# Strassen's scheme for most of the gate and up products of four feed-forward stages in a fused float32 model kernel

## The chip, the cores and the metric

One core of a Trainium2 chip runs one launch of a whole small model. The metric is the device time of a launch in microseconds (us). TensorE is called PE, VectorE DVE, ScalarE ACT, GpSimd POOL, SyncE SP.

## What is computed

256 tokens of width 1024 go through four transformer layers in float32. Each layer has attention (or a mixer of three branches) and then a feed-forward stage with a hidden width of 2816; the last two layers add a gated embedding. The change concerns the feed-forward stages:

```python
FFN_HIDDEN = 2816                                       # D_MODEL = 1024, SEQ = 256
h = rms_norm(x, ffn_norm[layer])
gate, up = jnp.split(h @ w_gate_up[layer], 2, axis=-1)  # 256 x 1024 by 1024 x 5632
x = x + (jax.nn.silu(gate) * up) @ w_down[layer]        # 256 x 2816 by 2816 x 1024
```

There are four of them: `w_gate_up[0]`, `w_gate_up[1]`, `w_gate_up_2[0]`, `w_gate_up_2[1]`, all of the same size.

## The kernel before

**Products.** PE multiplies in a rounded float32 (`F32R`). To keep the accuracy every operand is split in a high and a low part, and each block product is three matmuls (`mm3`, lines 250 to 252): high by high, high by low, low by high. Activations are the stationary operand (128 tokens), weights the moving one (128 x 512). `Weight.split` makes the two parts of a raw weight block of 128 x 1024: ACT copies it rounded into `wh` (line 236), DVE subtracts, `wl = wr - wh` (line 237, both inputs in SBUF). `split_T` (line 269 on) transposes activations on PE and makes their two parts, on ACT from PSUM and on DVE from PSUM.

**Feed-forward stage** (`ffn`, line 466 on). Gate and up weights are packed in eleven chunks; chunk c has 256 gate and the matching 256 up columns. `up(c)` loads and splits four weight blocks, and for each half t of the tokens runs `dense`: 8 parts of the inner width x 3 matmuls into one PSUM bank (`psb`). ACT takes Silu of the gate half (`sg`, line 483), DVE multiplies by the up half (`h`, line 485). `turn(c)` transposes `h` into `hth` and `htl` (lines 493 to 497). `down(c)` takes two blocks of `w_down` of 128 x 1024 each and accumulates into four PSUM banks that live for the whole stage (two `psd`, two `psm`). The order is up(c), turn(c-1), down(c-2); the last two chunks' down products come at the end, bank by bank, so that the first bank's sum can go on early.

**What sets the order.** The code gives a program order; a planner (a list scheduler with a time model of its own) puts the instructions of each engine into a fixed order from it. Loads are kept in program order on SP's queue. At run time each engine works through its own list in order and waits on semaphores. Buffers belong to tags with a fixed number each (`BUFS`, line 155); a tile waits until one of its tag is free: five raw blocks `wr`, five each of `wh` and `wl`, 14 of `rg`, 8 of `vv`, 2 of `acc`, 4 of `qkT`. POOL does small work: sums for the norms, rotary additions (line 419), the merging of the mixer's branches (line 1068); it takes no part in the feed-forward products.

Of the kernel before, what the change touches and what calls it, by code (L numbers as in the profile page):

```python
# [51 lines left out]
GU_CHUNKS = [_cols((256 * c, 256 * c + 256), (FFN + 256 * c, FFN + 256 * c + 256)) for c in range(11)]  # L52
# [95 lines left out]
def model(ctx: ExitStack, tc: tile.TileContext, A, out, taps=None):  # L148
# [67 lines left out]
    def raw_block(src, off, n):  # L216
        raw = tmp([BLK], "wr", "wr")
        load(raw[:, :n], bass.AP(tensor=src.tensor, offset=src.offset + off, ap=[[n, P], [1, n]]))
        return raw

    class Weight:
# [8 lines left out]
        def load(self, k0, m, n, off):  # L230
            return k0, m, n, raw_block(self.src, self.base + off, m * n)[:, :m * n]
# [233 lines left out]

    def ffn(nm, w_gu, gu_base, w_dn, dn_base, after):
# [6 lines left out]
        hT = {}  # L473

        def up(c):
            w = gu.get(c)
            hs = []
            for t in range(2):
# [7 lines left out]
                hs.append(h)  # L486
            return hs

        def turn(c, hs):
            pt = psb()  # L490
            for t in range(2):
                for j in range(2):
                    nc.tensor.transpose(pt[:, j * 256 + t * P:j * 256 + (t + 1) * P], hs[t][:, j * P:(j + 1) * P], ident)  # L493
            hi, lo = tmp([2, 256], "xt", "hth", F32R), tmp([2, 256], "xt", "htl", F32R)
            v = pt.rearrange("p (j t) -> p j t", j=2)
            nc.scalar.activation(hi, v, AF.Copy)
            nc.vector.tensor_tensor(lo, v, hi.bitcast(F32), op=ALU.subtract)
            hT[c] = (hi, lo)
# [3 lines left out]
        def down(c, toks, cols=(0, 1)):  # L502
            if c not in dw:
                dw[c] = dn.block(*dn.by[0][2 * c]) + dn.block(*dn.by[0][2 * c + 1])
            hi, lo = hT[c]
            for t in toks:
                ts = slice(t * P, (t + 1) * P)
                for n in cols:
                    for k, wh, wl in dw[c]:
                        j = k - 2 * c  # L510
                        s = slice(n * 512, n * 512 + 512)
                        mm3(acc[t, n], hi[:, j, ts], lo[:, j, ts], wh[:, s], wl[:, s], c == 0 and j == 0, c == 10 and j == 1)

        hs = {0: up(0)}
        for c in range(1, 11):
            hs[c] = up(c)
            turn(c - 1, hs.pop(c - 1))
            if c >= 2:
                down(c - 2, (0, 1))
        turn(10, hs.pop(10))  # L520
        for t in range(2):
            for n in range(2):
                down(9, (t,), (n,))
                down(10, (t,), (n,))
# [23 lines left out]
    def layer0(nm, after):  # L548
# [7 lines left out]
        vt = [tmp([3, 2, 65], "vv", "vt") for _ in range(2)]  # L556
# [8 lines left out]
        qp, qr, qb = ([tmp([2, 256], "rg", nm_) for _ in range(2)] for nm_ in ("qp", "qr", "qb"))  # L565
# [17 lines left out]
        def keys_T(dup):  # L583

            z = tmp([2, 256], "rg", "kz")
# [9 lines left out]
        def dup_tile(name):  # L595
            return tmp([2, 2, 64], "vv", name)
# [6 lines left out]
        ksd, kwd, bkd, kcd, vcd = [], [], [], [], []  # L603
        for t in range(2):
# [6 lines left out]
            kcd.append(dup_tile("kcd"))  # L611
# [6 lines left out]
        kz = {0: keys_T(ksd)}  # L618
# [49 lines left out]
        def chunk2():  # L668

            w = win.get(2)  # L670
# [678 lines left out]
```

## Time and profile before

| | |
|---|---|
| median of 3 runs | 1595.64 us (1594.61 to 1598.0) |
| the profiled run's own time | 1594.98 us |
| its span | 1593.1 us |
| instructions | 21691 |
| read from HBM | 267 MB, 168 GB/s over the span |
| loads of `w_gate_up` | 176 of 512 KB |

The profile is one execution. A row of busy time counts the time in which an engine has an instruction under way; matmuls are pipelined, so that two rows overlap, and the distance of their starts is the pace. "Idle before" is what the engine stood still ahead of an instruction, with what ended that. A weight load (PEld) overlaps the matmuls.

### The profile page before, as it was taken

The numbers are of one execution on the slowest core, as the hardware profiler recorded it, in microseconds if no ns is written. First come the engines' busy times: TensorE is split into PE (matmuls) and PEld (weight loads), VectorE is DVE, ScalarE is ACT, GpSimd is POOL, SyncE is SP. The second block draws the span as 40 slices with busy tenths as digits, with TensorE's granted clock in tenths as the row PEclk, the third lists the DMA queues.
The fourth block names the chain that finished last, engine by engine and source line by source line (L and its number), as shares of the span: only waits on it lengthen the run. The fifth ranks groups of instructions, "written<-read, shape, count | busy, mean of one in ns | idle before, by whom it ended". The sixth has DMA issues, their size and how long they took to land.

```text
span 1593.1 us, 21691 instructions
## 1 busy us (share of the span) xinstructions
PE 1561.7 (98%) x7870; PEld 1314.3 (82%) x7870; DVE 978.9 (61%) x1770; ACT 856.8 (54%) x1385; POOL 140.3 (9%) x231
## 2 busy tenths in 40 slices
PE   8999999999999999999999999999999999999997
PEld 7777888899888888798878888888898778888886
DVE  6685545577665555675686655457576776554556
ACT  5545444454554444676574654446675474644445
POOL 2010000011100000120023000000120023000001
PEclk9999999999999999999999999999999999999999
DMA  7424555544545565452556555564552555465661
GB/s 268 155 84 143 194 184 181 183 149 131 171 146 186 184 197 185 140 187 79 172 160 225 171 187 186 184 198 159 164 173 87 184 186 178 161 203 184 198 203 56
DMA packets 80588, 269.53 MB, mean 169 GB/s; under 512 B 11361, under 2 KB 12769, under 8 KB 80481
## 3 DMA queue, kind: packets, MB, share of 16 engines
q1 hardware_dynamic: 80048, 267.10, 51.6%
q8 instruction: 62, 1.02, 0.3%
q10 hardware_dynamic: 432, 1.05, 0.2%
q14 instruction: 46, 0.37, 0.1%
HBM read 267.06 MB, written 1.05 MB: 168 GB/s over the span
## 4 chain that ended last, share of the span: by engine, by line
PE 93%; DVE 3%; ACT 2%; issue 1%; DMA 1%; POOL 0%; POOLq 0%; SPq 0%; DVEq 0%; ACTq 0%
PE psd L250 14%; PE psd L252 14%; PE psd L251 14%; PE psb L252 10%; PE psb L250 10%; PE psb L251 10%; PE psb L357 5%; PE psm L251 3%; PE psm L250 3%; PE psm L252 3%; PE psb L374 1%; DVE wl L237 1%; PE psb L493 1%; PE psb L269 1%; PE psm L269 1%
## 5 line engine op out<-in xcount | busy, mean ns | idle before, releaser
L237 DVE TENSOR_TENSOR wl<-wr,wh 128x1024 fp32r<-128x1024 f32 (+2 forms) x504 | 596.7, 1197 | 425.1 <-ACT wh L236 411.1
L236 ACT ACTIVATE wh<-wr 128x1024 fp32r<-128x1024 f32 (+2 forms) x504 | 512.5, 1031 | 456.6 <-PE psb L252 176.9
L250 PE MATMUL psd<-wh,th 128*128 128x512 f32 (+4 forms) x888 | 336.1, 381 | 7.3 <-DVE gt L1049 5.2
L252 PE MATMUL psd<-wh,tl 128*128 128x512 f32 (+4 forms) x888 | 332.9, 376 | 3.4 <-DVE tl L278 3.4
L251 PE MATMUL psd<-wl,th 128*128 128x512 f32 (+4 forms) x888 | 333.3, 376 | 0.8 <-DVE wl L237 0.8
L252 PE MATMUL psb<-wh,tl 128*128 128x512 f32 x720 | 275.0, 390 | 0.0
L251 PE MATMUL psb<-wl,th 128*128 128x512 f32 x720 | 274.5, 389 | 0.0
L250 PE MATMUL psb<-wh,th 128*128 128x512 f32 x720 | 274.0, 390 | 0.0
L250 PEld LDWEIGHTS psd<-wh,th 128*128 128x128 f32 x888 | 167.5, 189 | 34.4 <-DVE gt L1049 4.5
L252 PEld LDWEIGHTS psd<-wh,tl 128*128 128x128 f32 x888 | 167.3, 188 | 29.4 <-DVE tl L278 5.0
L251 PEld LDWEIGHTS psd<-wl,th 128*128 128x128 f32 x888 | 167.5, 189 | 25.0 <-DVE wl L237 1.6
L252 PEld LDWEIGHTS psb<-wh,tl 128*128 128x128 f32 x720 | 135.2, 188 | 28.1
L251 PEld LDWEIGHTS psb<-wl,th 128*128 128x128 f32 x720 | 135.2, 188 | 28.0
L250 PEld LDWEIGHTS psb<-wh,th 128*128 128x128 f32 x720 | 135.2, 188 | 27.6
L305 POOL TENSOR_SCALAR rest<-ss 128x1 f32<-128x1 f32 x24 | 7.2, 301 | 919.0 <-ACT junk L315 919.0
L366 ACT ACTIVATE pr<-pr,m 128x128 f32<-128x128 f32 (+1 forms) x144 | 58.4, 449 | 40.7 <-DVE m L365 39.1
L250 PE MATMUL psd<-wh,hth 128*128 128x512 f32 x176 | 71.9, 412 | 0.0
L483 ACT ACTIVATE sg<-psb,r 128x256 f32<-128x256 f32 x88 | 41.9, 476 | 52.6 <-PE psb L252 52.5
L251 PE MATMUL psd<-wl,hth 128*128 128x512 f32 x176 | 68.8, 391 | 0.0
L251 PE MATMUL psm<-wl,hth 128*128 128x512 f32 x176 | 68.5, 389 | 0.0
L250 PE MATMUL psm<-wh,hth 128*128 128x512 f32 x176 | 68.5, 389 | 0.0
L252 PE MATMUL psm<-wh,htl 128*128 128x512 f32 x176 | 67.8, 389 | 0.0
(322 smaller groups left out, 1762.4 us busy)
## 6 DMA issues: line engine op xcount, KB each, us to landing
wr<-w_gate_up SPq DMA_DIRECT2D x176, 512.0 KB, 4.3
wr<-w_down SPq DMA_DIRECT2D x88, 512.0 KB, 3.3
wr<-w_in SPq DMA_DIRECT2D x88, 512.0 KB, 4.1
wr<-w_qkv_o SPq DMA_DIRECT2D x32, 384.0 KB, 3.4
wr<-w_o SPq DMA_DIRECT2D x16, 512.0 KB, 4.2
wr<-w_ple_gate SPq DMA_DIRECT2D x16, 512.0 KB, 3.8
wr<-w_in_e SPq DMA_DIRECT2D x10, 512.0 KB, 4.8
wr<-w_out_e SPq DMA_DIRECT2D x8, 512.0 KB, 4.7
```

Of the source, the lines that this page charges most:

```text
L236: nc.scalar.activation(hi[:, :m * n], raw, AF.Copy)
L237: nc.vector.tensor_tensor(lo[:, :m * n], raw, hi[:, :m * n].bitcast(F32), op=ALU.subtract)
L250: nc.tensor.matmul(o, xh, wh, start=start, stop=False)
L251: nc.tensor.matmul(o, xh, wl, start=False, stop=False)
L252: nc.tensor.matmul(o, xl, wh, start=False, stop=stop)
L269: nc.tensor.transpose(p[:, j * P:(j + 1) * P], src[:, j * P:(j + 1) * P], ident)
L305: nc.gpsimd.tensor_scalar(rest, ms, self.eps, None, op0=ALU.add)
L357: mm = lambda o, l, r, a, b: nc.tensor.matmul(o, l, r, start=a, stop=b, skip_group_check=True)
L366: exps.append(nc.scalar.activation(e, e, AF.Exp, bias=neg, scale=-1.0))
L374: nc.tensor.transpose(bank[j][:, b * P:(b + 1) * P], pr[:, j, b * P:(b + 1) * P], ident)
L483: nc.scalar.activation(sg, o[:, :256], AF.Silu, scale=r)
L493: nc.tensor.transpose(pt[:, j * 256 + t * P:j * 256 + (t + 1) * P], hs[t][:, j * P:(j + 1) * P], ident)
```

## The change

Eight of the eleven chunks are taken in four pairs. A pair has 512 gate and 512 up columns. With A the activations cut in two halves of tokens and two halves of the inner width, and B the pair's weights cut in two halves of the inner width and into gate and up, the four result blocks (two halves of tokens, gate and up) are made by Strassen's scheme (in Winograd's form): seven block products of 128 tokens x 512 inner x 512 columns in place of eight. Four of the seven weight operands are sums or differences of weight blocks (`t1` to `t4`), made by POOL (`combine`) ahead of the split; four activation operands are sums (`ms`), made once per stage (`mixed`: POOL adds, ACT and DVE split). The seven products share three PSUM banks, and ACT and DVE read partial sums between them. Parts 0, 5 and 6 of the seven `PARTS` stay as they were (`plain`). `down` goes by single blocks of 128 hidden columns, and `seven` and `plain` call `fill()` to place a `turn` or a `down` between two products.

For the room the buffer tags are cut anew: `rg`, `vv`, `acc`, `qkT` and `cm` become `ra` (7 buffers of 1024 columns) and `sb` (8). Attention and mixer tiles are taken from these two, most of them as a `duo`: two halves of one buffer, which come free together. Raw blocks of a pair come from `ra`, combined ones from `sb`.

```diff
+PARTS = [(0, 256), (256, 512), (768, 512), (1280, 512), (1792, 512), (2304, 256), (2560, 256)]
...
-    BUFS = {"wr": 5, "wh": 5, "wl": 5, "xt": 16, "rg": 14, "acc": 2, "w512": 5, "qkT": 4, "pr": 2, "pt": 2, "vv": 8, "fa": 4, "qk": 2, "ow": 2, "junk": 1, "cm": 1, "w128": 4}
+    BUFS = {"wr": 5, "wh": 5, "wl": 5, "xt": 16, "ra": 7, "sb": 8, "w512": 5, "pr": 2, "pt": 2, "fa": 4, "qk": 2, "ow": 2, "junk": 1, "w128": 4}
...
+    def duo(shape, tag, name, dt=F32):
+
+        t = tmp([2] + list(shape), tag, name, dt)
+        return [t[:, 0], t[:, 1]]
...
+    def combine(x, y, op):
+
+        k0, m, n, v = x
+        z = tmp([BLK], "sb", "wt")
+        nc.gpsimd.tensor_tensor(z, v, y[3], op=op)
+        return k0, m, n, z
...
+        def mixed():
+
+            f = lambda x: x.bitcast(F32)
+            tok = {}
+            for t, n in ((1, 0), (1, 1), (0, 0), (0, 1)):
+                hi, lo = nm.h[t, n]
+                tok[t, n] = tmp([4, P], "w512", "xa")
+                nc.gpsimd.tensor_tensor(tok[t, n], f(hi), f(lo), op=ALU.add)
+            s1, s2, s3, s4 = tok[1, 1], tok[0, 0], tok[1, 0], tok[0, 1]
+            nc.gpsimd.tensor_tensor(s1, tok[1, 0], tok[1, 1], op=ALU.add)
+            nc.gpsimd.tensor_tensor(s3, tok[0, 0], tok[1, 0], op=ALU.subtract)
+            nc.gpsimd.tensor_tensor(s2, s1, tok[0, 0], op=ALU.subtract)
+            nc.gpsimd.tensor_tensor(s4, tok[0, 1], s2, op=ALU.subtract)
...
+            for j, v in ((2, s2), (3, s3), (1, s1), (4, s4)):
+                hi, lo = ms[j] = to[j]
+                nc.scalar.activation(hi, v, AF.Copy)
+                nc.vector.tensor_tensor(lo, v, f(hi), op=ALU.subtract)
+
+        def product(o, x, blocks, start, stop):
+            w = sum((gu.split(b) for b in blocks), [])
+            for j, (_, wh, wl) in enumerate(w):
+                mm = [(x[0], wh), (x[0], wl), (x[1], wh)]
+                for e, (l, r) in enumerate(mm):
+                    nc.tensor.matmul(o, l[:, j, :], r, start=start and j == 0 and e == 0, stop=stop and j == 3 and e == 2, skip_group_check=True)
...
+            for e in range(2):
+                b11[e] = ld(g[e])
+            for e in range(2):
+                b12[e], b22[e] = ld(u[e]), ld(u[2 + e])
+            for e in range(2):
+                b21[e] = ld(g[2 + e])
+            for e in range(2):
+                t3[e] = combine(b22[e], b12[e], ALU.subtract)
+                t2[e] = combine(t3[e], b11[e], ALU.add)
+                t1[e] = combine(b12[e], b11[e], ALU.subtract)
+            for e in range(2):
+                t4[e] = combine(b21[e], t2[e], ALU.subtract)
+            r = nm.rstd
+            new = lambda: tmp([512], "w512", "hx")
+            A_, B_, F_ = psb(), psb(), psb()
+            product(A_, nm.h[0, 0], b11, True, False)
+            h0 = new()
+            nc.scalar.activation(h0, A_, AF.Copy)
+            fill()
+            product(B_, nm.h[0, 1], b21, True, True)
+            nc.vector.tensor_tensor(h0, h0, B_, op=ALU.add)
+            nc.scalar.activation(h0, h0, AF.Silu, scale=r[0])
+            if not ms:
+                mixed()
+            product(A_, ms[2], t2, False, False)
+            h1 = new()
+            nc.scalar.activation(h1, A_, AF.Copy)
+            fill()
+            product(F_, ms[3], t3, True, False)
+            product(A_, ms[1], t1, False, False)
+            u1 = new()
+            nc.scalar.activation(u1, A_, AF.Copy)
+            nc.vector.tensor_tensor(u1, u1, F_, op=ALU.add)
+            fill()
+            product(A_, ms[4], b22, False, True)
+            nc.vector.scalar_tensor_tensor(h0, A_, r[0], h0, op0=ALU.mult, op1=ALU.mult)
+            fill()
+            product(F_, nm.h[1, 1], t4, False, True)
+            nc.vector.tensor_tensor(h1, h1, F_, op=ALU.add)
+            nc.scalar.activation(h1, h1, AF.Silu, scale=r[1])
+            nc.vector.scalar_tensor_tensor(h1, u1, r[1], h1, op0=ALU.mult, op1=ALU.mult)
...
-            ksd.append(dup_tile("ksd"))
...
-        accA, accB = (tmp([2, 512], "acc", "acc") for _ in range(2))
+        accA, accB = (tmp([2, 512], "sb", "acc") for _ in range(2))
...
+            pw[0, n], pw[1, n] = duo([512], "ra", "pw")
...
-                pw[t, n] = tmp([512], "rg", "pw")
```

## Rows read from the trace of the kernel before

**Rows 1.** The page, part 1: busy us (share) x instructions
```profile
PE 1561.7 (98%) x7870; PEld 1314.3 (82%) x7870; DVE 978.9 (61%) x1770; ACT 856.8 (54%) x1385; POOL 140.3 (9%) x231
```
**Rows 2.** The page, part 4: the chain that ended last, by engine
```profile
PE 93%; DVE 3%; ACT 2%; issue 1%; DMA 1%; POOL 0%; POOLq 0%; SPq 0%; DVEq 0%; ACTq 0%
```
**Rows 3.** Windows of first and last feed-forward stage: PE, PEld, DVE, ACT, POOL; clock; DMA
```profile
143.00:329.00 186.00, 186.00 (x848) 153.93 (x847) 101.16 (x120) 89.39 (x121) 1.97 (x6) 1.00 0.56 184
...
1373.00:1559.00 186.00, 186.00 (x845) 153.87 (x844) 98.48 (x108) 88.86 (x114) 0.98 (x3) 1.00 0.58 190
```
**Rows 4.** Waits of the first feed-forward stage: us, times, longest
```profile
DVE wl L237 <- ACT wh L236: 74.2, 30, 4.0
...
ACT wh L236 <- PE psb L252: 43.4, 30, 4.3
```
**Rows 5.** Timeline of PE in the first stage: start us, us, instruction
```profile
203.66 0.39 PE L250 MATMUL psb<-wh,th 128*128 128x512 f32 x1
...
204.34 0.62 PE L250 MATMUL psb<-wh,th 128*128 128x512 f32 x2
```
**Rows 6.** The chain in that stage, longest pieces: start us, us
```profile
204.51 0.45 PE psb L250 x2
...
238.11 0.45 PE psb L250 x2
```
**Rows 7.** Groups of DVE by form: busy us, mean ns, idle before
```profile
L237 DVE TENSOR_TENSOR wl<-wr,wh 128x1024 fp32r<-128x1024 f32 x442 | 536.3, 1226 | 392.9 <-ACT wh L236 379.1
...
L526 DVE TENSOR_TENSOR x<-x,psd 128x512 f32<-128x512 f32 x8 | 5.5, 688 | 1.6 <-PE psd L252 1.6
...
L1139 DVE SCALAR_TENSOR_TENSOR ug<-ug,rgt 128x512 f32<-128x512 f32 x4 | 2.5, 668 | 0.0
```
**Rows 8.** Groups of ACT by form
```profile
L236 ACT ACTIVATE wh<-wr 128x1024 fp32r<-128x1024 f32 x442 | 461.8, 1059 | 413.6 <-PE psb L252 176.9 <-PE psm L252 145.5 <-PE psd L252 80.3
...
L928 ACT ACTIVATE u<-psd,r 128x512 f32<-128x512 f32 x4 | 2.8, 691 | 9.8 <-PE psd L252 9.8
```
**Rows 9.** Timeline of POOL: additions of 128 and 512 columns; 512 with one source
```profile
41.58 0.46 POOL L419 TENSOR_TENSOR kr<-ra,rb 128x128 f32<-128x128 f32 x1 [0.67 <-DVE rb L418]
...
818.71 1.04 POOL L1133 TENSOR_TENSOR rgt<-xc 128x512 f32<-128x512 f32 x1 [0.88 <-ACT xc L1130]
...
853.56 1.29 POOL L1068 TENSOR_TENSOR gt<-gt 128x512 f32<-128x512 f32 x1 [28.06 <-DVE gt L1064]
```
**Rows 10.** Timeline: POOL starts just after `wl`
```profile
873.50 1.22 DVE L237 TENSOR_TENSOR wl<-wr,wh 128x1024 fp32r<-128x1024 f32 x1
873.73 2.13 POOL L1068 TENSOR_TENSOR gt<-gt 128x512 f32<-128x512 f32 x1 [2.52 <-DVE gt L1064]
```
**Rows 11.** Timeline: `wl` starts just after POOL
```profile
718.22 0.46 POOL L419 TENSOR_TENSOR qtok<-ra,rb 128x128 f32<-128x128 f32 x1 [4.18 <-DVE rb L418]
718.28 1.48 DVE L237 TENSOR_TENSOR wl<-wr,wh 128x1024 fp32r<-128x1024 f32 x1
```
**Rows 12.** Timeline: a DVE operation that reads PSUM while POOL works
```profile
862.36 3.46 POOL L1068 TENSOR_TENSOR gt<-gt 128x512 f32<-128x512 f32 x2 [1.99 <-DVE gt L1064]
863.39 0.69 DVE L1064 TENSOR_TENSOR gt<-psd,gt 128x512 f32<-128x512 f32 x1
```
**Rows 13.** Timeline at the start of the first stage
```profile
142.84 11.92 SPq L176 DMA_DIRECT2D wr<-w_gate_up  x5
...
147.67 2.15 DVE L278 SCALAR_TENSOR_TENSOR tl<-psm,S,th 128x128 fp32r<-128x128 f32 x8
```
**Rows 14.** The page, part 6: loads, KB each, us to landing
```profile
wr<-w_gate_up SPq DMA_DIRECT2D x176, 512.0 KB, 4.3
```
**Rows 15.** Windows (columns as in rows 3) and timeline around a wait in a mixer
```profile
1296.00:1300.00 4.00, 2.04 (x9) 1.40 (x8) 4.00 (x7) 4.00 (x7) 0.00 (x0) 1.00 0.18 74
1300.00:1304.00 4.00, 4.00 (x12) 3.09 (x12) 4.00 (x8) 1.62 (x4) 0.00 (x0) 0.57 0.64 166
...
1299.23 0.50 PE L250 MATMUL psd<-wh,th 128*128 128x512 f32 x1 [1.96 <-DVE gt L1049]
```

More of the change, by code (lines that the diff above doesn't have):

```diff
@@ L51 @@
 ] + [_cols((3240 + 512 * j, 3752 + 512 * j)) for j in range(6)]
-GU_CHUNKS = [_cols((256 * c, 256 * c + 256), (FFN + 256 * c, FFN + 256 * c + 256)) for c in range(11)]
+PARTS = [(0, 256), (256, 512), (768, 512), (1280, 512), (1792, 512), (2304, 256), (2560, 256)]
+GU_CHUNKS = []
+for _a, _n in PARTS:
+    _g, _u = (_a, _a + _n), (FFN + _a, FFN + _a + _n)
+    GU_CHUNKS += [_cols(_g, _u)] if _n == 256 else [_cols(_g), _cols(_u)]
 HALVES = [_cols((0, 512)), _cols((512, 1024))]
@@ new lines, in product, with seven @@
+        def product(o, x, blocks, start, stop):
[4 more added lines that the diff above has]
+                    nc.tensor.matmul(o, l[:, j, :], r, start=start and j == 0 and e == 0, stop=stop and j == 3 and e == 2, skip_group_check=True)
+        def seven(i, c, fill):
+            g, u = gu.by[c], gu.by[c + 1]
+            ld = lambda b: gu.load(*b, tag="ra")
+            b11, b12, b21, b22, t1, t2, t3, t4 = ([None, None] for _ in range(8))
+            for e in range(2):
[34 more added lines that the diff above has]
+            nc.vector.scalar_tensor_tensor(h0, A_, r[0], h0, op0=ALU.mult, op1=ALU.mult)
+            fill()
+            product(F_, nm.h[1, 1], t4, False, True)
+            nc.vector.tensor_tensor(h1, h1, F_, op=ALU.add)
+            nc.scalar.activation(h1, h1, AF.Silu, scale=r[1])
+            nc.vector.scalar_tensor_tensor(h1, u1, r[1], h1, op0=ALU.mult, op1=ALU.mult)
+            hs[i] = [h0, h1]
@@ L506, in down, with turn @@
+        def turn(i):
+            n = PARTS[i][1] // P
+            hT[i] = [split_T(h, n) for h in hs.pop(i)]
+        dw = {}
+        def down(i, k, toks, cols):
+            if k not in dw:
+                dw[k] = dn.block(*dn.by[0][k])[0][1:]
+            wh, wl = dw[k]
+            j = k - PARTS[i][0] // P
             for t in toks:
-                ts = slice(t * P, (t + 1) * P)
+                hi, lo = hT[i][t]
                 for n in cols:
[L509 to L520, printed above, removed]
+                    s = slice(n * 512, n * 512 + 512)
+                    mm3(acc[t, n], hi[:, j, :], lo[:, j, :], wh[:, s], wl[:, s], k == 0, k == FFN // P - 1)
+        def kts(i):
+            return [(i, k) for k in range(PARTS[i][0] // P, sum(PARTS[i]) // P)]
+        end = kts(len(PARTS) - 2) + kts(len(PARTS) - 1)
@@ new lines, in ffn, with fill @@
+        c = 0
+        for i, (a, n) in enumerate(PARTS):
+            todo = []
+            if i:
+                todo.append(lambda: turn(i - 1))
+            if i > 0:
+                todo += [lambda i_=i_, k=k: down(i_, k, (0, 1), (0, 1)) for i_, k in kts(i - 1) if (i_, k) not in end]
+            def fill():
+                if todo:
+                    todo.pop(0)()
+            (plain if n == 256 else seven)(i, c, fill)
+            while todo:
+                fill()
+            c += 1 if n == 256 else 2
@@ L521, in ffn @@
+        turn(len(PARTS) - 1)
         for t in range(2):
             for n in range(2):
-                down(9, (t,), (n,))
-                down(10, (t,), (n,))
+                for i, k in end:
+                    down(i, k, (t,), (n,))
                 s = slice(n * 512, n * 512 + 512)
@@ L555, in layer0 @@
         load(w2v, A["cmp_v_w2"])
-        vt = [tmp([3, 2, 65], "vv", "vt") for _ in range(2)]
+        vt = duo([3, 2, 65], "sb", "vt")
         for t in range(2):
@@ L670, in chunk2 @@
             w = win.get(2)
+            kwd, bkd = (dup_tiles(n_) for n_ in ("kwd", "bkd"))
             for t in range(2):
@@ L987, in branch @@
         def branch(qt, kt, v, dk, mask):
-            o = tmp([2, 512], "acc", "acc")
+            o = tmp([2, 512], "sb", "acc")
             for j in range(4):
-                s = [heads_T(lambda t: qt(t, 2 * j + h), lambda t: kt(t, 2 * j + h), dk) for h in range(2)]
+                s = duo([2, 256], "ra", "qkT")
+                for h in range(2):
+                    heads_T(s[h], lambda t: qt(t, 2 * j + h), lambda t: kt(t, 2 * j + h), dk)
                 pov, _ = attend(lambda h: s[h][:dk, 0], lambda h: s[h][:dk, 1], lambda kt_, h: v[kt_][:, 2 * j + h, :], mask)
@@ L1075, in mixer @@
         sigmoids = gate(2, of_attention)
-        uT = [tmp([2, 259], "vv", "uT") for _ in range(2)]
+        uT = duo([2, 259], "sb", "uT")
         for a in range(2):
@@ L1080, in mixer @@
         channels(5, lambda a, t, v: nc.vector.tensor_copy(uT[a][:, :, 3 + t * P:3 + (t + 1) * P], v))
-        ug = [tmp([2, 256], "rg", "ug") for _ in range(2)]
+        ug = duo([2, 256], "ra", "ug")
         channels(6, lambda a, t, v: nc.vector.tensor_copy(ug[a][:, :, t * P:(t + 1) * P], v))
-        bds = []
+        bds = duo([4, P], "ra", "bd")
         for a in range(2):
-            bd = tmp([4, P], "qkT", "bd")
+            bd = bds[a]
             fill(bd, 0.0)
```

90 lines of the change are left out of this document (36 added, 54 removed).

## The prediction

> **What bounds the kernel now.** I read the page from the top: PE is busy 1561.7 of 1593.1 us, DVE 61%, ACT 54%, POOL 9% [rows 1], and the chain that ended last is 93% PE [rows 2]. The windows of the four feed-forward stages show PE busy for all of their 186 us, DVE for 98 to 101, POOL for 1 to 2 (first and last stand in [rows 3], the two between are like them). In those stages the waits run back to PE: DVE waits for ACT's high parts, ACT waits for PE to free them [rows 4]. So there a matmul taken away is time taken away, as long as nothing else becomes the last.
>
> A matmul's row says 0.39 us, but the rows overlap: the fourth start lies 0.68 us after the first (203.66, 204.34) [rows 5], 0.2265 each. That pace is the price. The same row comes back after two chunks at 238.11 instead of 204.51 [rows 6]: 33.6 us for a pair of chunks, which is 96 gate and up matmuls, 48 down matmuls (144 x 0.2265 = 32.6) and 8 transposes (1.0).
>
> The profiled run took 1594.98 us, 1.88 over its span and 0.66 under the median shown; the sum is made on 1594.98.
>
> **What is removed.** A pair goes from 96 to 7 x 12 = 84 gate and up matmuls. 12 x 0.2265 = 2.72 us per pair, so PE needs 30.9 instead of 33.6; four pairs make 10.9 us per stage, 16 pairs 43.5 us. Down matmuls, transposes and weight bytes stay as many; the order of operands inside a product is that of `dense`, so the pace should stay.
>
> **What is added, engine by engine, per pair.** The gate and up weights were split 8 times per pair, now 14 (two blocks for each of seven products), plus 4 down blocks as before: 18.
> - DVE: 18 x 1.23 = 22.1, and seven of 512 columns (two `tl`, five on the products) x 0.69 = 4.8 [rows 7]: 26.9 us.
> - ACT: 18 x 1.06 = 19.1, and seven of 512 columns (two high parts, three copies, two Silu) x 0.69 = 4.8 [rows 8]: 23.9 us.
> - POOL: eight `combine`s of 1024 columns. No row has that size. 128 columns take 0.46, 512 take 1.29 [rows 9]: about 2.2 ns a column, so 2.4 us each (between 2.1 and 2.6: twice 1.04, the 512-column row with one source, and twice 1.29, [rows 9]) and 19 us for eight.
>
> Each alone is under 30.9. The catch is that DVE and POOL do not run side by side here. When `wl` (two SBUF inputs) runs first, POOL's 512-column addition, started 0.23 later, takes 2.13 instead of 1.29 and ends 1.14 after `wl` ended [rows 10]. When POOL runs first (718.22, 0.46 long), `wl` started at 718.28 takes 1.48 instead of 1.23 and ends 1.08 after POOL ended [rows 11]. A DVE operation that reads PSUM is not held: `gt<-psd,gt` keeps its 0.69 beside a POOL addition [rows 12]. So the two queue for one path, each for nearly its whole length. The Trainium skill ("SBUF — State Buffer", Who interferes with whom) says the same: a DVE instruction with two SBUF inputs and a GpSimd one that reads SBUF exclude each other for a whole instruction, one with a single SBUF input excludes nothing. By that rule all PSUM readers could hide and the sum would be the low end below; were it not to hold, the sum would be the first rival.
>
> The price of the path per pair:
> - 18 `wl` x 1.08 = 19.4 (end of POOL to end of `wl` [rows 11]);
> - the last product `h1`, two SBUF inputs, about 0.6 (L1139, 0.67 [rows 7], less its start);
> - 8 combines x 2.27 = 18.2 (1.14 from the end of `wl` to the end of POOL [rows 10], plus 512 more columns x 2.2 ns = 1.13).
>
> Together 38.2 us against PE's 30.9: the path is the new bound inside a pair. Two things can come on top. DVE's six PSUM readers (4.1 us) hide only while POOL holds the path, about half of the time: I take 2.05. A combined block goes POOL, ACT, DVE, so its high part (1.06 [rows 8]) is exposed where DVE stands in order at its `wl`: I take one per pair, the bounds are none and two. Taken: 38.2 + 2.05 + 1.06 = 41.3; bounds 38.2 and 44.4.
>
> **The first pair of a stage.** `mixed` adds eight POOL operations of 512 columns (8 x 1.15 = 9.2 on the path) and four `wl`-like subtractions of 512 (4 x 0.6 = 2.4): 11.6. It needs all of the norm, whose last DVE parts run at 147.67 to 149.8 [rows 13], 5 us into the stage, and product three waits for it. Chunk 0 brings four `wl` (4.3). Pair one has two down blocks fewer (-2.2). Combines may start before the stage's first matmul: its first loads are issued as raw buffers come free from 142.84 on and land in 4.3 us [rows 13, 14]; I take two combines ahead (-4), bounds none and four (-9).
>
> **The sum per stage.** Chunk 0 and four pairs on the path: 4.3 + 11.6 + 4 x 41.3 - 2.2 - 4 = 174.9. What follows (two plain chunks and the last down products) stays PE's: 186 - 10.9 = 175.1 in all, less chunk 0 (48 x 0.2265 = 10.9), pair one (30.9 less two down blocks of 2.72 and 0.5 of transposes: 25.0) and three pairs (92.7), leaves 46.5; there DVE has a `wl` per 2.7 us of PE. Stage: 221.4 instead of 186, +35.4; four stages +142. **1594.98 + 142 = 1737 us.** Low: 4.3 + 11.6 + 152.8 - 2.2 - 9 + 46.5 = 204.0, +18.0, 1667. High: 4.3 + 11.6 + 177.6 - 2.2 + 46.5 = 237.8, +51.8, 1802.
>
> **Buffers.** The tags `rg`, `vv`, `acc`, `qkT`, `cm` become `ra` (7) and `sb` (8), with two halves freed together. In a pair eight raw blocks share `ra`; in the second block's stages `pw` holds two, so five are left and `b22` lies until product six. From there to the next pair's second product runs a chain: load 4.3 [rows 14], combine, load, combine, load, about 13 + 5 = 18 us or up to 20 behind `wl`s, and the path itself takes nine `wl` (9.7) and some five combines (11.4) over that stretch: it just hides. Cover gone, it costs at most a landing per pair, 8 x 4.3 = 34 us in the two later stages; I count 0. A blocked load holds later ones on SP's queue, the down weights among them; these were loaded ahead by five raw buffers. In attention and mixer I take 0 too: a gain can be no more than PE's idle 31.4 us [rows 1], a loss about one landing in each of four stages, 17 us. Six `sb` buffers are left for the eight combined blocks (two hold `m` for the stage), which also keeps POOL from working far ahead.
>
> **The rivals.**
> *The path costs nothing, PE stays last* (the other side). Place: `wl` beside `combine`. If POOL's additions fit into DVE's pauses, 43.5 us come back, less the wait for `mixed` in product three, say 5 us x 4 stages: about 1572, and 1551 without that wait. It decides where a combine holds the path for less than (30.9 - 20.0) / 8 = 1.36 us. For it: each engine alone has room. Against it: [rows 10, 11] show the whole length held, which leaves 2.27.
> *The path's work spreads over the whole stage.* 90 `wl` x 1.08 + 32 x 2.27 + 11.6 + 2.4 = 184, almost the 186 of before: about 1590. Against it: a combine can't run a pair ahead with six buffers.
> *PE's clock falls in the new pauses.* Waiting a quarter of the time, PE may lose its level: one wait of 1.96 us at 1299.23, in a stretch with PE busy for 2.04 of 4.00 us, is followed by a granted clock of 0.57 in the next 4 us, part of them at the 1.2 GHz level [rows 15]. The Trainium skill ("TensorE: Matmul & The Clock Gate", HAM oscillation) warns of just this pattern, waits between bursts that throttle it again and again; the rows agree on one such fall. Each such fall costs 4 x (1 - 0.57) = 1.7 us; PE has 10 us of slack per pair, so only badly placed ones count: three per pair uncovered, 16 x 5.1 = 82, about 1819. For it: a single wait stood before that fall. Against it: a slower PE has less slack, and so fewer pauses.
> *The change doesn't do what it says*: the counts of matmuls are fixed by the code, so I give it nothing.
>
> **How the numbers follow.** Forecast (the path bounds the pairs) 0.77, own range 1667 to 1802; clock or load chain on top (above 1802) 0.10; PE stays last 0.08; spread 0.05. The range reaches down by 17 us for what the buffers may give and up by 13 for part of the next case: 1650 to 1815. A measurement can tell 0.2%, 3.2 us, from no change: faster 0.09, same 0.03, slower 0.88.
>
> **What would show it.** Right: in the pairs' stretch `wl` has a mean well above 1.23 (toward 1.7 to 2.2), `combine` one of 2.5 to 3.5, DVE is busy near 90 to 100% there, PE below 85%, waiting for `wl`; the pairs lie about 41 us apart and chunks 5 and 6 run at 16.8 as before. Wrong: `wl` at 1.23 beside POOL, pairs 31 us apart, PE still at 100%. The load chain would show as POOL waiting for DMA in the last two stages only, the clock as a granted share well under 1. The weakest numbers are the combine's length, which no row has, and how much of the PSUM work hides.

## The result and the profile after

The changed kernel takes 1834.07 us (median of 4 runs, 1825.01 to 1838.59), 1595.12 before: 1.149 times as long (95% interval 1.144 to 1.153). The forecast had 1737 us, with 1650 to 1815 as its range: the direction held, and the loss is 239 us where 142 were worked out. The profiled run of after took 1835.5 us, 1833.5 of it span, so the sum below is 240.4 us of span against before.

**Where the time lies.** I cut both traces at the same instructions, the last addition into `x` at the end of each stage. The attention and mixer parts reach to that addition, the feed-forward parts from there to the next. In the third and fourth the gated embedding's input lies inside.

| stretch, us | before | after | difference | forecast |
|---|---|---|---|---|
| first attention | 143.8 | 157.2 | +13.4 | 0 |
| feed-forward 1 | 185.0 | 221.2 | +36.2 | +35.4 |
| second attention | 127.9 | 140.6 | +12.8 | 0 |
| feed-forward 2 | 185.4 | 219.0 | +33.6 | +35.4 |
| first mixer | 255.5 | 265.0 | +9.5 | 0 |
| feed-forward 3 | 190.4 | 253.6 | +63.2 | +35.4 |
| second mixer | 280.8 | 288.9 | +8.2 | 0 |
| feed-forward 4 | 190.4 | 254.0 | +63.6 | +35.4 |
| end | 34.0 | 34.0 | 0 | 0 |

So the first two stages came out as forecast. The miss of 98 us (240.4 of span against 142) is in two other places: 56 in the two later stages, 44 in attention and mixers.

The page after, part 1 (busy us, share, instructions), then part 4 (the chain that ended last, by engine), then three groups of part 5; they answer to [rows 1, 2, 7]:

```profile
PE 1616.9 (88%) x7678; PEld 1325.0 (72%) x7678; DVE 1318.3 (72%) x1910; ACT 986.9 (54%) x1525; POOL 576.0 (31%) x391
...
PE 62%; DVE 13%; POOL 10%; issue 7%; DMA 5%; ACT 4%; POOLq 0%; DVEq 0%; ACTq 0%
...
L480 POOL TENSOR_TENSOR wt<-wr 128x1024 f32<-128x1024 f32 x64 | 189.8, 2966 | 209.5 <-DMA wr<-w_gate_up 144.6
...
L247 DVE TENSOR_TENSOR wl<-wt,wh 128x1024 fp32r<-128x1024 f32 x128 | 221.7, 1765 | 9.7 <-ACT wh L246 9.1
...
L480 POOL TENSOR_TENSOR wt<-wt,wr 128x1024 f32<-128x1024 f32 x32 | 97.4, 3043 | 4.5 <-issue 2.4
```

PE is no longer the whole chain (93% before). DVE, POOL and the loads hold 28% of it. PE has 192 matmuls fewer and is busy for 55 us longer, which goes with a lower granted clock (mean 0.928, before 0.995). The `wl` of combined blocks takes 1.77 us on average instead of 1.23, and these combines 3.0 us.

Windows of the four feed-forward stages after, columns as in [rows 3]:

```profile
157.00:378.00 221.00, 191.09 (x790) 149.82 (x789) 189.89 (x151) 117.00 (x146) 105.47 (x43) 0.94 0.42 145
520.00:739.00 219.00, 188.29 (x797) 149.19 (x796) 190.92 (x151) 119.89 (x151) 100.03 (x40) 0.94 0.42 144
1003.00:1257.00 254.00, 202.40 (x820) 158.50 (x819) 179.81 (x151) 124.87 (x156) 104.14 (x46) 0.85 0.39 135
1546.00:1800.00 254.00, 201.34 (x819) 157.54 (x818) 176.45 (x150) 124.59 (x156) 105.24 (x46) 0.86 0.40 137
```

DVE's work nearly doubles, from 101 to 190 us. In the later two stages DVE is busy for less in a longer time, so there the path between DVE and POOL isn't what makes them longer than the first two. What the engines wait for says it. Waits of the first stage (157 to 378 us) and of the third (1003 to 1257), in us, times, longest; the first three lines are the first stage's, the last two SP's own queue in the third:

```profile
POOL wt L480 <- DVE wl L247: 33.4, 4, 12.3
...
POOL wt L480 <- DMA wr<-w_gate_up: 16.5, 3, 8.5
...
PE psb L531 <- DVE wl L247: 8.3, 7, 2.2
...
ACT wh L246 <- DMA wr<-w_gate_up: 43.9, 7, 12.2
POOL wt L480 <- DMA wr<-w_gate_up: 43.8, 7, 17.8
...
PE psb L531 <- ACT wh L246: 33.7, 10, 6.8
...
SPq L186 <- DVE wl L247: 122.0, 35, 26.7
SPq L186 <- POOL wt L480: 103.1, 13, 13.8
```

In the first stage PE's longest wait in all is for `wl`, as forecast: 8.3 us in the pairs of the 30 us that PE stands idle, the rest in small waits on DVE and ACT. In the third, ACT and POOL wait for weight loads, and the loads wait in SP's queue for a combine to free a raw block: 103.1 us, where it is 39.3 in the first stage. The queue's waits for a `wl` are no longer than there (122.0 against 142.0).

**The shared path at work.** Windows of the second and third pair of the first stage and of the second pair of the second, columns as in [rows 3]; then the timeline of POOL and of DVE in the third pair of the first stage (start us, us, instruction):

```profile
213.00:253.00 40.00, 34.29 (x141) 26.81 (x140) 37.66 (x27) 22.18 (x25) 22.47 (x9) 0.91 0.43 143
253.00:297.50 44.50, 34.83 (x142) 26.11 (x140) 44.14 (x25) 22.41 (x26) 31.45 (x10) 0.96 0.48 174
572.00:614.00 42.00, 34.46 (x140) 26.72 (x139) 39.59 (x26) 22.34 (x25) 26.02 (x9) 0.92 0.51 180
...
275.36 3.34 POOL L480 TENSOR_TENSOR wt<-wr 128x1024 f32<-128x1024 f32 x1
278.78 3.26 POOL L480 TENSOR_TENSOR wt<-wt,wr 128x1024 f32<-128x1024 f32 x1
282.00 3.36 POOL L480 TENSOR_TENSOR wt<-wr 128x1024 f32<-128x1024 f32 x1
...
276.36 11.23 DVE L247 TENSOR_TENSOR wl<-wr,wh 128x1024 fp32r<-128x1024 f32 x4
```

DVE is busy for 94 to 99% of a pair, PE for 78 to 86%. In the timeline DVE and POOL take turns. A combine starts every 3.2 to 3.4 us, with one `wl` in between, where the forecast's price was 1.08 + 2.27 = 3.35. Four `wl` last 11.23 us instead of 4 x 1.23.

**The loads at work.** Timeline of POOL, of ACT and of PE in a pair of the third stage; the brackets hold the idle time ahead and what ended it:

```profile
1076.79 2.34 POOL L480 TENSOR_TENSOR wt<-wr 128x1024 f32<-128x1024 f32 x1 [3.60 <-DMA wr<-w_gate_up]
...
1082.47 2.34 POOL L480 TENSOR_TENSOR wt<-wr 128x1024 f32<-128x1024 f32 x1
1095.26 2.40 POOL L480 TENSOR_TENSOR wt<-wr,wt 128x1024 f32<-128x1024 f32 x1 [10.45 <-DVE wl L247]
...
1088.32 1.06 ACT L246 ACTIVATE wh<-wr 128x1024 fp32r<-128x1024 f32 x1 [9.29 <-DMA wr<-w_gate_up]
...
1089.43 0.80 PE L531 MATMUL psb<-wh,th 128*128 128x512 f32 x1 [6.58 <-ACT wh L246]
```

The second block of `b21`, the operand of product two, can be loaded only when a combine frees a raw block: that of 1082.47 ends at 1084.81, the load goes out at 1084.84 and lands at 1088.24, and ACT goes on at 1088.32. The combined blocks' high parts stand behind `b21`'s on ACT, so DVE stands too, and POOL waits for DVE to free `sb`. ACT does nothing for 9.3 us, PE for 6.6.

**Attention at work.** Windows of the first and the second attention, before, then after, cut at the end of that last addition into `x`:

```profile
0.00:144.40 144.40, 132.77 (x840) 110.69 (x841) 99.45 (x331) 76.34 (x167) 19.72 (x38) 0.98 0.46 159
329.50:457.30 127.80, 126.42 (x762) 113.77 (x760) 92.68 (x237) 65.72 (x131) 19.40 (x30) 1.00 0.44 141
...
0.00:157.80 157.80, 142.54 (x842) 118.63 (x843) 104.42 (x331) 79.70 (x176) 33.20 (x42) 0.94 0.46 160
379.00:519.60 140.60, 135.14 (x765) 120.50 (x764) 93.10 (x238) 67.68 (x134) 34.24 (x36) 0.94 0.47 154
```

Nearly the same matmuls keep PE busy for 18.5 us more in the two, at a granted clock of 0.94 instead of 0.98 and 1.00, and PE stands idle for 8 us more. In the two mixers it is busy for 5.2 us more (clock 0.98 instead of 1.00 and 0.99) and idle for 12 more.

### The profile page after: what moved, and what is told of

The parts are those of the page before. It is cut to its first block, busy times and chain, and to the rows that moved or that the text cites. A ratio compares the mean times of both kernels' runs of the same rounds, so it can differ in the third digit from the quotient of the medians.

```text
span 1833.5 us, 21803 instructions
## 1 busy us (share of the span) xinstructions
PE 1616.9 (88%) x7678; PEld 1325.0 (72%) x7678; DVE 1318.3 (72%) x1910; ACT 986.9 (54%) x1525; POOL 576.0 (31%) x391
## 4 chain that ended last, share of the span: by engine, by line
PE 62%; DVE 13%; POOL 10%; issue 7%; DMA 5%; ACT 4%; POOLq 0%; DVEq 0%; ACTq 0%
PE psd L261 11%; PE psd L262 11%; PE psd L260 11%; DVE wl L247 10%; POOL wt L480 8%; PE psb L531 7%; PE psb L367 5%; DMA wr<-w_gate_up 4%; PE psb L262 2%; PE psb L260 2%; PE psb L261 2%; ACT wh L246 2%; PE psm L261 2%; PE psm L260 2%; PE psm L262 2%
## 5 line engine op out<-in xcount | busy, mean ns | idle before, releaser
L480 POOL TENSOR_TENSOR wt<-wr 128x1024 f32<-128x1024 f32 x64 | 189.8, 2966 | 209.5 <-DMA wr<-w_gate_up 144.6
L247 DVE TENSOR_TENSOR wl<-wt,wh 128x1024 fp32r<-128x1024 f32 x128 | 221.7, 1765 | 9.7 <-ACT wh L246 9.1
L246 ACT ACTIVATE wh<-wt 128x1024 fp32r<-128x1024 f32 x128 | 133.5, 1053 | 55.3 <-PE psb L531 25.1
L531 PE MATMUL psb<-wh,th 128*128 128x512 f32 x192 | 86.3, 451 | 69.1 <-ACT wh L246 69.1
L480 POOL TENSOR_TENSOR wt<-wr,wt 128x1024 f32<-128x1024 f32 x32 | 91.3, 2858 | 116.3 <-DVE wl L247 102.3
L315 POOL TENSOR_SCALAR rest<-ss 128x1 f32<-128x1 f32 x24 | 10.1, 421 | 360.8 <-ACT junk L325 360.8
L531 PE MATMUL psb<-wl,th 128*128 128x512 f32 x192 | 87.5, 456 | 33.4 <-DVE wl L247 33.4
L531 PEld LDWEIGHTS psb<-wh,th 128*128 128x128 f32 x192 | 40.5, 211 | 85.2 <-ACT wh L246 77.3
L531 PE MATMUL psb<-wh,m 128*128 128x512 f32 x256 | 89.1, 409 | 13.9 <-ACT m L523 7.5
L480 POOL TENSOR_TENSOR wt<-wt,wr 128x1024 f32<-128x1024 f32 x32 | 97.4, 3043 | 4.5 <-issue 2.4
L531 PE MATMUL psb<-wh,tl 128*128 128x512 f32 x192 | 83.9, 437 | 0.0
L262 PE MATMUL psb<-wh,tl 128*128 128x512 f32 x208 | 81.9, 395 | 1.4 <-DVE tl L288 1.4
L260 PE MATMUL psb<-wh,th 128*128 128x512 f32 x208 | 82.4, 399 | 0.0
```

The lines of the kernel that those rows point to most:

```text
L246: nc.scalar.activation(hi[:, :m * n], raw, AF.Copy)
L247: nc.vector.tensor_tensor(lo[:, :m * n], raw, hi[:, :m * n].bitcast(F32), op=ALU.subtract)
L260: nc.tensor.matmul(o, xh, wh, start=start, stop=False)
L262: nc.tensor.matmul(o, xl, wh, start=False, stop=stop)
L315: nc.gpsimd.tensor_scalar(rest, ms, self.eps, None, op0=ALU.add)
L480: nc.gpsimd.tensor_tensor(z, v, y[3], op=op)
```

## The experiments

All medians are of four runs; the kernel before took 1595.9 to 1597.3 us beside them.

**1. Short combines.** To take the path away and leave nearly all else: few columns added, POOL's time filled by writes alone.

```diff
-        nc.gpsimd.tensor_tensor(z, v, y[3], op=op)
+        nc.gpsimd.tensor_tensor(z[:, :32], v[:, :32], y[3][:, :32], op=op)
+        for _ in range(2):
+            nc.gpsimd.memset(z[:, 32:], 0.5)
```

> Edit: a combine reads 32 columns of its two operands and POOL then only writes the other 992 columns, twice over, so that it is busy about as long (0.25 + 2 x about 0.95, from the 0.52 us of a 512-column MEMSET) but hardly reads SBUF. The combined blocks are wrong but for 32 columns. Theory (DVE and POOL queue for one read path): wl falls from 1.42 to about 1.23 us in the mean, pairs lie 31 to 35 us apart in the first two stages, these fall from 221 and 219 us to about 185; the last two, where loads are late as well, fall by less; 1834 becomes 1690 to 1730. Rival (the combined blocks simply come late from POOL, whatever DVE does): pairs stay 40 to 45 us apart, the time within 20 us of 1834.

Measured: 1650.28 us, ratio 1.034 (1.030 to 1.038), less than the theory's 1690 to 1730. The first two stages take 187.6 and 186.9 us, as it had them. Window of the third pair of the first stage:

```profile
233.00:264.00 31.00, 31.00 (x142) 25.66 (x141) 25.94 (x26) 22.75 (x25) 19.81 (x24) 1.00 0.48 178
```

POOL is busy for 19.8 of 31 us, as it was forecast to be, PE is full and the pair lasts 31.0 us. POOL's being busy costs nothing; that it reads SBUF beside DVE does. In this stretch `wl` means 1.22 to 1.24 us. With the path gone the later stages also fall, from +63 to +11.4 and +6.5. A short combine also ends its reading of a raw block after 0.25 to 1.3 us, so these come free sooner; for the later stages the run doesn't part the two.

**2. Half combines**, 512 columns added and 512 written over. By the forecast's price this path is 38.2 - 8 x 1.13 = 29.2 us, just under PE's 30.9.

```diff
-        nc.gpsimd.tensor_tensor(z, v, y[3], op=op)
+        nc.gpsimd.tensor_tensor(z[:, :512], v[:, :512], y[3][:, :512], op=op)
+        nc.gpsimd.memset(z[:, 512:], 0.5)
```

> Edit: a combine adds 512 of its 1024 columns; POOL only writes the others (0.52 us). The other half of each combined block is wrong. Theory (path): a combine holds the path for 1.14 us, under the 1.36 from which the prediction said it decides, so 19.4 + 0.6 + 8 x 1.14 = 29.1 us per pair, under PE's 30.9; with what DVE can't hide (2 to 5 us) pairs lie 31 to 36 us apart in the first two stages, and the time is nearer to the 1650 of the run without the path than to 1834: 1670 to 1710. Rival (the loss grows in proportion to POOL's length, no point from which it decides): half way, about 1742.

Measured: 1707.69 us, ratio 1.068 (1.064 to 1.073). Windows of the second and third pair of the first stage:

```profile
200.20:232.10 31.90, 31.18 (x141) 25.57 (x140) 31.77 (x26) 22.66 (x26) 17.32 (x16) 1.00 0.58 200
232.10:263.30 31.20, 31.20 (x142) 25.62 (x141) 31.18 (x25) 22.20 (x25) 19.09 (x16) 1.00 0.56 202
```

DVE is busy all the time, its `wl` stretched to 1.58 us (combined blocks) and 1.67 us (raw ones), and PE nearly so: both are at their limit, and the pairs take 31.9 and 31.2 (32.6 and 33.1 in the second stage). Half the combine does not cost half the loss (that would be pairs of 36 to 37): at a path of 29.2 us a pair is 0.2 to 2.2 us longer than with none, at 38.2 it is 9 to 14 longer. The bound changes between the two, where the forecast had put it, at 30.9. The time is 57 us over experiment 1 all the same; between the profiled runs 43 of 53 us lie in the two later stages, where the loads are late.

**3. Combines on DVE.** One engine, no sharing: 18 x 1.21 + 8 x 1.22 + 7 x 0.69 = 36.4 us of DVE a pair.

```diff
-        nc.gpsimd.tensor_tensor(z, v, y[3], op=op)
+        nc.vector.tensor_tensor(z, v, y[3], op=op)
```

> Edit: the eight combines of a pair are done by DVE instead of POOL. Theory of the shared path: a combine takes 1.2 us of the path instead of 2.27, so a pair needs 26.9 + 8 x 1.2 = 36.5 us of DVE; pairs 37 to 39 us apart in the first two stages, about 5 us less in each of 16 pairs, 1834 - 80 = about 1755. Rival (DVE's own length of queue is the limit and POOL only a helper): DVE gets 9.6 us more per pair, pairs 45 us or more apart, 1834 or more.

Measured: 1716.87 us, ratio 1.075 (1.073 to 1.077). The theory had about 1755, with pairs 37 to 39 us apart. Windows of the second and third pair of the first stage, and one group of DVE:

```profile
201.40:232.30 30.90, 29.72 (x133) 24.09 (x132) 30.28 (x31) 21.61 (x25) 0.00 (x0) 1.00 0.50 175
232.30:267.60 35.30, 33.43 (x141) 26.57 (x140) 35.24 (x35) 22.65 (x26) 0.00 (x0) 0.95 0.53 196
...
L480 DVE TENSOR_TENSOR wt<-wr 128x1024 f32<-128x1024 f32 x64 | 77.8, 1219 | 10.8 <-DMA wr<-w_gate_up 10.7
```

A combine takes 1.22 us on DVE and costs 2.27 of the path on POOL. So POOL is not help but harm here: the work costs the path more there than if DVE did it alone, and 117 us come back. DVE is busy throughout, as the theory had it, with 31 and 35 operations in the two pairs in place of 33. The pairs are shorter than expected, and the stages fall by 25 to 33 us each where 20 were worked out; where the rest comes from wasn't looked for.

**4. The gated embedding's input after the stage**, so that its two `pw` buffers don't sit in `ra` while the pairs run.

```diff
-        pw = ple_input(i)
         ffn(nf, A["w_gate_up_2"], i * D * 2 * FFN, A["w_down_2"], i * FFN * D, norm_after(npl))
+        pw = ple_input(i)
```

> Edit: in the last two layers the embedding product pw is made after the feed-forward stage, not before it, so that its two ra buffers are free during the stage (seven for the pairs' raw blocks instead of five). Theory (a chain of loads that wait for ra buffers costs the 28 us that stages three and four lose beyond stages one and two): both fall from 254 to 222 to 228 us, 1834 - 56 = about 1778. Rival (the clock, at 0.85 there, or the order of work): they stay within 8 us of 254.

Measured: 1803.84 us, ratio 1.128 (1.124 to 1.132). Window of the third stage, to be read beside 254 us, PE 202 and clock 0.85:

```profile
1000.00:1221.00 221.00, 182.00 (x774) 142.51 (x773) 193.44 (x142) 119.53 (x150) 114.20 (x46) 0.95 0.40 143
```

Stages three and four take 221.1 and 223.7 us, as the theory had them, and like the first two; the time falls by 30 us only, where 56 were expected. Of each stage's fall (32.5 and 30.3 us) 5.4 us is the input's own work, now elsewhere (by as much these stages are longer already before, 190.4 against 185.0); the other 27 and 25 us were the load chain, with the clock's fall that came with it, nearly all of the 28 by which each of these stages had passed the first two. What follows the stage loses part of the gain: second mixer +24.0 and end +11.9, where after had +8.2 and 0. Of these 15.8 and 11.9 us, 5.4 each are the moved work; the rest was not traced.

**5. Two plain chunks first**, to give the norm, `mixed` and the first combines time.

```diff
-PARTS = [(0, 256), (256, 512), (768, 512), (1280, 512), (1792, 512), (2304, 256), (2560, 256)]
+PARTS = [(0, 256), (256, 256), (512, 512), (1024, 512), (1536, 512), (2048, 512), (2560, 256)]
...
-        end = kts(len(PARTS) - 2) + kts(len(PARTS) - 1)
+        end = kts(len(PARTS) - 1)
```

> Edit: two plain parts stand ahead of the four pairs and one behind them (before: one and two); the last part's down products alone come at the end. Theory (a stage's start is bound by mixed and the first combines on the path; product three of pair one starts 28 to 38 us after product one): POOL gets 10.9 us of PE's time more to work ahead in, each stage falls by 5 to 11 us, 1834 becomes 1790 to 1815. Rival (the path is full whatever the order): within 8 us of 1834.

Measured: 1820.0 us, ratio 1.140 (1.138 to 1.143): 14 us, under the theory's 19 to 44 and over the rival's 8. The first two stages even take 5 to 7 us more each than after's, the last two 10 less: 7.6 us gained in the four. Another 10.1 of the 18.7 us between the two profiled runs lie in the first attention. So late combines at a stage's start aren't what costs the first two stages. That POOL can't work ahead into the plain chunks by more than its buffers would explain it, but wasn't shown.

**6. Two plain chunks first and short combines.**

> Edit: that of the run without the path (combines read 32 columns, POOL writes the rest, wrong but for these) with two plain parts ahead of the pairs. There the first pair took 39 to 46 us and the others 31. Theory (that first pair waits for mixed and for the first combined blocks): its distance falls to 25 to 33 us, four stages give 10 us each, 1650 becomes about 1610; stages one and two fall under the 185 us of before. Rival (the first pair is held by something else, PSUM banks or the order): unchanged, 1640 to 1660.

Measured: 1659.05 us, ratio 1.039 (1.037 to 1.040). The time is the rival's, the first pair still took 36 to 42 us; experiment 7 shows that `mixed` held it all the same, from the place where the code calls it. Timeline of POOL in it, then of PE:

```profile
175.84 7.99 POOL L515 TENSOR_TENSOR xa<-th,tl 128x512 f32<-128x512 f32 x4
183.79 2.25 POOL L517 TENSOR_TENSOR xa<-xa 128x512 f32<-128x512 f32 x1
...
190.55 1.60 POOL L520 TENSOR_TENSOR xa<-xa 128x512 f32<-128x512 f32 x1
...
188.97 0.77 PE L533 MATMUL psb<-wh,m 128*128 128x512 f32 x1 [2.34 <-ACT m L525]
```

`mixed` starts only when the first pair has begun (174.6), where the code calls it, though two plain chunks have run on the norm's parts before. Its eight additions take 16.3 us (175.84 to 192.15), where the forecast had 9.2: seven of the eight are near 2 us, beside a `wl` of DVE, as the 2.13 in [rows 10] had shown.

**7. The same with `mixed` ahead of the second plain chunk.**

```diff
         for i, (a, n) in enumerate(PARTS):
...
+            if i == 1:
+                mixed()
             (plain if n == 256 else seven)(i, c, fill)
```

> Two plain chunks first and short combines as in the run before it of that kind (32 columns added, the rest written over by POOL, so the combined blocks hold other values), and in addition the mixed activations are made ahead of the second plain chunk instead of inside the first pair. That run took 1659 us, and its first pairs lasted 36.2, 36.1, 41.0 and 41.7 us where the second ones lasted 31.7 to 32.5. If the mixed activations hold the first pair (eight POOL additions that took 16.3 us from 175.84 to 192.15 in place of the 9.2 forecast, with product three waiting for them), the first pairs fall to about 32: 1659 - 4.5 - 4.4 - 9 - 9 = about 1632 us. If loads or the first combined blocks hold product three, the first pairs stay as they are: 1655 to 1660 us.

Measured: 1615.95 us, ratio 1.011 (1.006 to 1.015), 43 us less where 27 were expected. The first pairs now last 25 to 26 us (they have fewer `down` blocks), the others mostly 31, and the stages end 6.8, 8.4, 3.3 and 5.2 us earlier than before the change: at last what seven products in place of eight are worth, of 10.9 forecast. The second pair of stages three and four still takes 36.8 and 34.6.

**8. The same early `mixed`, combines whole.**

> The same move of the mixed activations, ahead of the second plain chunk, with the combines whole (all blocks right), beside the run of two plain chunks first, 1820 us. If the shared path of DVE and POOL sets the pairs' pace, the mixed work only leaves the first pairs as far as these are longer than the others (50.5 and 45.9 us against 42 in the first two stages, no longer than the others in the last two): about 1808 us, 1800 to 1815. If the mixed work costs its 16 us on POOL in every stage, 1775 to 1795.

Measured: 1806.5 us, ratio 1.130 (1.127 to 1.133). Against experiment 5 the first two stages give 6 us each and the last two 0 to 1, as the first expectation had it, with a path that is full in the pairs that follow. Windows of its first two stages:

```profile
154.00:374.00 220.00, 183.74 (x789) 141.35 (x789) 203.60 (x151) 118.55 (x155) 116.69 (x46) 1.00 0.44 156
513.00:733.00 220.00, 191.05 (x796) 149.53 (x795) 200.68 (x151) 119.92 (x155) 115.17 (x46) 0.95 0.45 158
```

The first stage has its clock at 1.00, the second at 0.95 in the mean, and PE is busy for 7 us more there. Both take 220.4 to 220.5 us.

**9. All chunks plain**, with the new buffer tags and the new order of the code.

```diff
-PARTS = [(0, 256), (256, 512), (768, 512), (1280, 512), (1792, 512), (2304, 256), (2560, 256)]
+PARTS = [(256 * c, 256) for c in range(11)]
```

> Edit: all eleven parts plain, 256 columns each, no pairs, no combines; the new buffer tags and the new order of down products stay. It computes the reference. If the new tags themselves cost what attention and mixer lost (13.4 + 12.8 + 9.5 + 8.2 = 44 us): these stretches keep their loss and the time is about 1640. If it is the pairs' raw blocks, loaded early into ra and kept there, or combines started early: the stretches are back within 2 us each and the time is 1590 to 1603.

Measured: 1628.51 us, ratio 1.021 (1.018 to 1.023). The stages are as long as before to 0.1 us; 32 us are lost in attention and mixers (+3.1, +11.9, +9.6, +7.4), with no Strassen product in the kernel. Waits of PE in the first mixer, then the window of the second attention, to be read beside that of before (busy for 126.4 us, clock 1.00):

```profile
PE psd L260 <- ACT wh L246: 5.6, 1, 5.6
PE psm L1211 <- issue: 2.3, 1, 2.3
...
332.00:471.00 139.00, 133.52 (x760) 119.29 (x758) 90.68 (x234) 66.18 (x130) 18.20 (x30) 0.94 0.40 129
```

**10 and 11. One tag at a time**, all chunks plain. In 10 the tiles of `sb` are single again, in 11 those of `ra` (there with 14 `rg`).

```diff
     def duo(shape, tag, name, dt=F32):
...
+        if tag == "sb":
+            return [tmp(shape, "vv", name, dt) for _ in range(2)]
...
```

> All eleven chunks plain, and of the new tags only `ra` (with `qkT` in it): the tiles of `sb` are taken singly again, eight `vv` and two `acc`. The run with all chunks plain and both new tags took 1628.5 us, 32 over the kernel before: 3.1 in the first attention, 11.9 in the second, 9.6 and 7.4 in the mixers. If it is the sharing of `sb` (sums, values and the LRU's tiles come free later, in pairs) that costs this, about 1598 to 1604 us. If it is `ra` (rotated queries, keys, transposed keys, gates in halves), 1622 to 1630. If each holds its own part, between.

> All chunks plain, and of the new tags only `sb`: the tiles of `ra` are taken singly again, 14 `rg` (with the `qkT` ones among them). If the sharing of `sb` costs the 32 us, 1622 to 1630 us. If it is `ra`, 1598 to 1604 us. If each holds its own part, between.

Measured: 1619.54 us, ratio 1.015 (1.013 to 1.016), and 1628.96 us, 1.020 (1.017 to 1.023). Window of the second attention in 10:

```profile
333.00:460.00 127.00, 125.62 (x759) 113.13 (x757) 91.78 (x234) 64.85 (x129) 19.37 (x30) 1.00 0.43 141
```

With `sb` single the second attention is as before (127.9 us, +0.0) and its clock is back at 1.00: there it was the shared buffers of `sb`. In 11 it loses 15.0. The first attention and the mixers keep their loss in both (+4.0, +12.1 and +10.0 in 10; +3.0, +9.6 and +7.4 in 11). So taking back one tag alone does not cure them. Either each of the two tags is enough for the loss, or it comes from the new order of the code, which both runs keep. In 9 the wait of 5.6 us is for a high part that ACT has in its list behind the work of one of the mixer's branches (tile `lru`), and that waits for POOL; in 10 PE waits 6.3 us for POOL's `lru` itself. Both would fit a changed order of the planner. The old tags with the new code weren't run, and the cause stays open.

**12. What the single gains give together**: combines on DVE, the embedding's input late, two plain chunks first.

> Edit: combines on DVE, embedding product made after the stage, two plain parts ahead of the pairs; it computes the reference. If the three effects add: 1717 - 20 to 30 for the late embedding product - 20 to 40 for the order = 1650 to 1675, still slower than before, since DVE's 36.5 us per pair is over the 33.6 of a pair before and the tags' 32 us stay. If they overlap: 1690 to 1710.

Measured: 1693.35 us (1676.94 to 1694.08), ratio 1.058 (1.052 to 1.063): the gains overlap. `mixed` early isn't in it. No version here beats the kernel before. Even with combines that cost nearly nothing and `mixed` early (experiment 7) the 24 us that the stages gain don't pay for the 45 that attention and mixers lose.

## Why the prediction was right on the direction and short on the size

The loss came, and in the first two stages it had the size and the cause that were forecast. The whole lies in the case to which I had given 0.10, "clock or load chain on top". Two steps failed: the cover of the load chain, and the nothing for attention and mixers.

**The bound, right.** PE was the bound and the path became it. Pairs two and three of the first two stages lie 40.2, 44.5, 42.4 and 44.0 us apart against 41.3 taken; turns of 3.2 to 3.4 us against 3.35. Experiments 1 and 2 show it from both sides. The pace of 0.2265 is 0.2267 by its own rows (0.68 / 3), which moves nothing. The Trainium skill ("SBUF — State Buffer", Who interferes with whom) has a DVE instruction with two SBUF inputs contend with a GpSimd one that reads SBUF, and not with one that only writes it. This case's trace agrees with both: turns of 3.2 to 3.4 us, and in experiment 1 a `wl` of 1.22 to 1.24 us beside 14.4 us of writes.

**A stage's sum, right in part by luck.** 221.2 us against 221.4 looks better than it is. In the first stage the stretch to the second pair took 55.5 us (51.0 forecast), two pairs 84.8 (82.6), the last pair 32.7 (41.3) and what follows 48.3 (46.5). The last pair has no combines of a next one beside it; I had put eight on each. The first pair with `mixed`, the pairs' distance and the end were too low by about as much: `mixed`'s additions took 12 to 16 us, 9.2 forecast.

**The rival that PE stays last, refuted in its own terms.** It decided below 1.36 us of path per combine. A combine of half the size, at 2.27 - 1.13 = 1.14, indeed left the pairs of the first two stages at 31 to 33 us. At the full length, 2.27, they were 40 to 44.

**Buffers in the later stages: the step that failed.** I saw the chain (`pw` holds two of seven, load, combine, load) and took it as hidden, since the path itself would work through nine `wl` and five combines meanwhile. But that work hangs on the same loads: `b21` stands first in ACT's list, the combined blocks behind it, so the cover waits with what it should cover. It cost 28 us a stage, 56 in all, where I counted 0, and over my bound of 34, which had priced one landing a pair; each gap is a combine, an issue and a landing. Experiment 4 takes it away.

**Attention and mixers: the second failed step.** I bounded the loss by one landing in each of four stages, 17 us, and counted 0. It is 44 in after, and 32 with the new tags and the new order of the code alone (experiment 9). I had looked at the tags as buffers for loads. They also release two halves together: in the second attention the loss is gone once the tiles of `sb` are single (experiment 10). What causes the rest is open. The kind of loss was missed too. By the windows, PE stands idle for only 20 us more in the four stretches; the other 24 us it is busy for longer. That is the size of the clock's fall there, an estimate from lengths and granted clocks: 157.8 x 0.06 + 140.6 x 0.06 + 265 x 0.02 + 289 x 0.02 = 29.0 after, less 144.4 x 0.02 + 280.8 x 0.01 = 5.7 before, gives 23. I had priced the clock in the pairs alone, where PE has slack; in attention PE has little, so 20 us of waits came to 44 with the lower clock. The 10 us by which the first attention is longer in after than in experiment 9 are mostly this too (PE busy for 142.5 us at 0.94, for 134.5 at 0.99); what began that fall isn't shown.

**The clock.** It did fall in the pairs (0.94, 0.94, 0.85 and 0.86 in the four stages), and 1819 was near the time, but for another reason: the trace has 17 stretches at the lower level in the four stages, about one a pair and not three. Where PE has slack the fall cost nothing: in experiment 8's first stage it is absent, and that stage is no shorter than its second, which has it. In attention, as said, it did cost. In the gaps of the load chain it is not clearly free. The windows around the gap above:

```profile
1076.00:1082.00 6.00, 2.45 (x5) 1.67 (x6) 1.23 (x1) 1.06 (x1) 5.13 (x2) 0.50 0.22 89
1082.00:1100.00 18.00, 11.27 (x34) 8.20 (x34) 10.59 (x9) 9.13 (x10) 6.34 (x4) 0.61 0.54 197
1100.00:1119.00 19.00, 19.00 (x85) 15.51 (x83) 19.00 (x11) 10.04 (x10) 11.34 (x4) 1.00 0.29 91
```

At 0.50, the 1.2 GHz level, PE enters the stretch after the gap; it is back at 1.00 only by 1100. How much of the 28 us a stage is waiting and how much is the lower level isn't separated: in experiment 4 both go together (in the third stage PE is busy for 20 us less, 5.4 of it moved work, and idle for 12 less).

**The spread over the whole stage, rightly given little.** POOL waited 33 us of the first stage for DVE to free `sb`, and experiment 5 gave 14 us of 1834, about half of it outside the stages.

## What to carry to other kernels

Before work goes to an idle engine, ask what it reads beside whom: a helper that shares a path with the bound engine can cost more than if the bound engine did the work itself (2.27 us against 1.22 here), and it costs little until the path is as long as the other bound, then about all that it is longer. Work counts as cover for a load only if it doesn't wait for the same load, in the order in which the engines hold it. When a change recuts buffers, time the new cut alone first: here it cost 32 us, with the code's new order, without the change that it was made for. And price a lower clock where the engine has no slack, not only where the change is: here it was more than half of what attention and mixers lost.

## What was not expected of the hardware

Three things that the rows of before did not show. A POOL instruction that only writes SBUF does not hold DVE's two-input operation: 14.4 us of writes in a pair of experiment 1 left `wl` at 1.22 to 1.24 us. Tiny POOL additions, on the other hand, are held up too: with 32 columns they took 0.25 us alone, and mostly 0.6 to 1.3 where a `wl` was under way. And a fall of the clock by itself need be no loss: two equal stages at 1.00 and at 0.95 took 220.5 and 220.4 us, with the path of DVE and POOL as the bound.
